# Sample states updated by VectorE beside the output and channel products, in a hybrid attention decoder layer

## Chip, cores and metric

The kernel runs on one NeuronCore of a Trainium2 chip. The metric is the device time of one execution in microseconds (us). TensorE is called PE below, its weight loads PEld, VectorE DVE, ScalarE ACT, GpSimd POOL, and SyncE, which issues nearly all DMAs, SP.

## What is computed

One decoder layer for 256 prompt tokens and 8 samples of 4 tokens each (288 tokens together), all in float32, model width 2048. After an RMSNorm, one input projection gives the operands of two branches and their gates. Branch A is sliding-window attention. Branch B is gated linear attention (GLA) with 4 heads, key width 256, value width 512 and a matrix state of 256 x 512 per head. For the samples, the states come in as an input and go out updated:

```
def step(S, xs):                      # one chunk; for a sample one chunk is its 4 tokens
    qc, kc, vc, dc = xs
    o = einsum('blhk,bhkv->blhv', qc, S)
    S = dc[..., None] * S + einsum('blhk,blhv->bhkv', kc, vc)
    return S, o
...
y = sigmoid(gs) * (o_swa @ p_swa) + sigmoid(gg) * (o_g @ p_gla)
x = x + y @ w_o
h2 = rms_norm(x, norm2)
x = x + square(relu(h2 @ w_up)) @ w_down
```

There are 8 samples x 4 heads = 32 sample states of 512 KB each. The state is used twice: `o` needs the product of the queries with the old state, and the new state is the decayed old one plus the sum over 4 tokens of key times value.

## The kernel before

All arrays are kept transposed, features on the 128 partitions and the 288 tokens along the free axis. All large products go through `gemm`. One `gemm` makes 512 output features; its weights come in chunks of 512 KB (`raw`, 128 x 1024, six buffers, loaded at L228 by SP), each chunk being two halves of 128 input rows. `wsplit` parts each half into a high part (`whi`, a rounding copy by ACT at L213) and a remainder (`wlo`, a subtraction by DVE at L155), five buffers of each. PE then does 24 matmuls for a chunk (L246): 2 halves x 4 output blocks x 3 products (high x high, high x low, low x high), all in the rounded float32 format. The four output banks (`mm`, four buffers) are read out by an `evac` function when the last chunk has been multiplied. The gemms follow each other in a fixed order: the input projections, `ps0..3` (attention's projection), more input projections (`gg`, `rg`: the gates), `pg0..3` (GLA's projection), `wo0..3` (output), and then four blocks of `up` and `dn` (the channel products), four gemms each.

All other work is put between chunks. `queues[0]` and `queues[1]` hold generators; after each chunk `pump(rate)` adds a rate to each queue's credit and runs one step (up to the next `yield`) of that queue for each whole credit. `gla(h)` is the prompt part of head h on queue 0; `gla_sample(h)` is its sample part on queue 1. The issue order on each engine is then set by the framework's scheduler, which takes what is ready by its own reckoning, the earliest traced first; `keep_in_program_order` pins an instruction behind the one traced before it on its engine.

`gla_sample(h)` does, before the change: the head's sample values in four copies are turned by PE (L787) and parted into `vs`; decays are made by ACT (`es`); the keys are weighted in four copies (`kdr`), turned by PE (L813) and parted into `kh`; then, two samples at a visit, two old states are loaded into `raw` buffers (L823), multiplied by the padded queries into the bank `pos` (L841), and for each of the two samples the keys of that sample are masked (`km`, L847, DVE), two matmuls make the new contribution (`pu`, L851) and DVE adds it to the decayed state in place (L852), which SP writes out (L853). After the four visits one matmul adds the part of the tokens within the sample (L855). Where the prompt part of the same head has its products ready (`tiled`), they are emitted beside a visit's matmuls. At the end the head's output is normalised by `rsqrt_mean` (L276 to L281), whose logarithm and exponential need another ACT function table than the sigmoids of `rg_evac` (L932); for head 3 `exp_table()` (L180) loads it, pinned.

The state writes and loads share SP's queue and the `raw` buffers with the weights.

Of the kernel before, what the change touches and what calls it, by code (L numbers as in the profile page):

```python
# [19 lines left out]
P = 128  # L20
D = 2048
KT = 16
TP = 256
# [5 lines left out]
GATE = 1.0 / 16.0  # L29
NEG = -1e30  # L30
# [100 lines left out]
def step_kernel(ctx: ExitStack, tc: tile.TileContext, a: dict):  # L131
# [36 lines left out]
    raw0 = main.tile([P, 1024], F32, name="raw", tag="raw", bufs=6)  # L168
# [48 lines left out]
    def gemm(name, xh, xl, evac, rate=(), first=None):  # L217
        nk = 2 * chunks_of(name)
        ps = [pmm.tile([P, 512], F32, name="mm", tag="mm") for _ in range(4)]
        for c in range(nk // 2):  # L220
            if FIRST[name] + c == 0:
                raw = raw0
            else:
                raw = main.tile([P, 1024], F32, name="raw", tag="raw", bufs=6)
# [12 lines left out]
            turns = c == nk // 2 - 1 or c == 0 and first is None  # L237
            order = [(i, m) for m in range(4) for i in range(2)] if turns else [(i, m) for i in range(2) for m in range(4)]
            order = [(i, m, j) for i, m in order for j in range(3)]
            if c == 0 and first is not None:  # L240

                order[:12] = [(0, m, j) for j in range(3) for m in range(4)]
            for i, m, j in order:
                k, hi, lo = parts[i]
                o, sl = ps[m][:, :NT], slice(m * P, m * P + P)
                T.matmul(o, lhsT=(lo if j == 2 else hi)[:, sl], rhs=xl(k) if j == 1 else xh(k),  # L246
                         start=k == 0 and j == 0, stop=k == nk - 1 and j == 2)
                if k == nk - 1 and j == 2:
                    evac(m, o)
            pump(rate)  # L250
# [14 lines left out]
    def rsqrt_mean(accs, n, out, ps=None):  # L265
# [10 lines left out]
        S.activation(t, ps[:, :NT], AF.Ln, scale=1.0 / n, bias=epst)  # L276
        V.tensor_scalar(m, ps[:, :NT], 1.0 / n, EPS, ALU.mult, ALU.add)
        S.activation(out, t, AF.Exp, scale=-0.5)
# [106 lines left out]
    def swa(pool):  # L385
        rope = pool.tile([P, 2, NT], F32, name="rope")
        vc1 = pool.tile([P, NB, P], F32, name="vc1")
# [119 lines left out]
        vc = [main.tile([P, NB, P], F32, name="vc0", tag="Zb3"), vc1]  # L507
# [73 lines left out]
    zqk, zv, og, ready, done, last_operands, tiled = {}, {}, {}, {}, set(), [], []  # L581
# [27 lines left out]
    ats = gpool.tile([P, 64], F32R, name="ats")  # L609
    V.memset(qm, 0.0)  # L610
    V.memset(f(ats), 0.0)
    bmask, amask, ii = bm[:, 32:32 + NB], bm[:, 0:32], bm[:, 32 + NB:64 + NB]
# [13 lines left out]
    def gla(h):  # L626
# [9 lines left out]
        vr = gpool.tile([P, 4, 4, TS], F32, name="vr")  # L636
        G.tensor_copy(vr, zv[h][:, :, TP:NT].unsqueeze(2).broadcast_to([P, 4, 4, TS]))
# [9 lines left out]
        ready[h] = (vr, pfx)  # L647
# [87 lines left out]
        tiled.append((products, lambda: cross(1)))  # L735
        for _ in range(8):
            if tiled:
                yield
# [40 lines left out]
    def gla_sample(h):  # L779
        zk = lambda t: zqk[h][:, 2 + t]  # L780
        while h not in ready:
            yield
        vr, pfx = ready[h]
        vs = gpool.tile([P, 512], F32R, name="vs")
# [3 lines left out]
        S.copy(vs, pv)  # L788
        sub(vs[32:64], pv[32:64], f(vs[32:64]))
        sub(vs[96:128], pv[96:128], f(vs[96:128]))  # L790
        yield
        ps = pfx[:, :, TP:NT]
# [9 lines left out]
        kdr = gpool.tile([P, 2, 4, TS], F32, name="kdr")  # L802
        mul(qi, zqk[h][:, 0:2, TP:NT], es[:, :, 0:TS])
        mul(kir, zqk[h][:, 2:4, TP:NT], ens)
        for t in range(2):
            kb = zk(t)[:, TP:NT].unsqueeze(1).broadcast_to([P, 4, TS])
            mul(kdr[:, t], kb, es[:, t, TS:64].unsqueeze(1).broadcast_to([P, 4, TS]))
        qd = qm.rearrange("p a (b c) -> p a b c", c=36)
        S.copy(qd[:, :, :, 0:NS], qi.rearrange("p a (b c) -> p a b c", c=NS))
        yield  # L810
        pk = bank("pks")
        for t in range(2):
            T.transpose(pk[:, P * t:P * t + P], kdr[:, t].rearrange("p a b -> p (a b)"), ident)  # L813
        kh = gpool.tile([P, 256], F32R, name="kh", tag="kh")
        S.copy(kh, pk[:, :256])
        sub(kh[64:128], pk[64:128, :256], f(kh[64:128]))
        yield
        pos = pos_.tile([P, 512], F32, name="pos", tag="pos")
        for b0 in range(0, NB, 2):
            st = []  # L820
            for b in (b0, b0 + 1):
                raw = main.tile([P, 1024], F32, name="raw", tag="raw", bufs=6)
                SY.dma_start(raw, a["s0"][h, b])  # L823
                st.append(raw)
            if b0 == 0:

                pa2 = bank("pa2")
                for t in range(2):
                    for g in range(4):
                        T.matmul(pa2[32 * g:32 * g + 32, :TS], lhsT=kir[:, t], rhs=qi[:, t], start=t == 0, stop=t == 1)  # L830
                at2 = gpool.tile([P, TS], F32, name="at2")
                mul(at2, pa2[:, :TS], amask)
                S.copy(ats[:, 0:TS], at2)
                sub(ats[64:128, 0:TS], at2[64:128], f(ats[64:128, 0:TS]))
            beside = tiled.pop() if tiled else (lambda: None, lambda: None)
            beside[0]()

            for g in range(2):
                for t in range(2):
                    r = 32 * (2 * g + t)  # L840
                    T.matmul(pos[r:r + 32], lhsT=qm[:, t, 32 * (b0 + g):32 * (b0 + g) + 32],  # L841
                             rhs=st[g][:, 512 * t:512 * t + 512], start=b0 == 0, stop=b0 == NB - 2 and r >= 64)
            beside[1]()
            for g in range(2):
                b, raw = b0 + g, st[g]
                km = gpool.tile([P, 256], F32R, name="km", tag="km")
                V.tensor_scalar(km, f(kh), bmask[:, b:b + 1], None, ALU.mult)  # L847
                for t in range(2):
                    rt = raw[:, 512 * t:512 * t + 512]
                    pu = bank("pu")  # L850
                    T.matmul(pu, lhsT=km[:, P * t:P * t + P], rhs=vs, start=True, stop=True)  # L851
                    V.scalar_tensor_tensor(rt, rt, es[:, t, NS * b + NS - 1:NS * b + NS], pu, ALU.mult, ALU.add)  # L852
                SY.dma_start(a["ssn"][h, b], raw)  # L853
                yield
        T.matmul(pos[:64], lhsT=ats, rhs=vs, start=False, stop=True)  # L855
# [24 lines left out]
        if h == 3:  # L880
            exp_table()
        rsqrt_mean([acc], 512, rso)
# [8 lines left out]
    R = (1.0, 0.55)  # L891
# [23 lines left out]
    R3 = (0.9, 0.55)  # L915
# [8 lines left out]
    for h in range(4):  # L924
# [3 lines left out]
        def rg_evac(m, ps):  # L928
# [6 lines left out]
            S.copy(gh[h][:, m], tt[:, m])  # L935
        gemm(f"rg{h}", H, L, rg_evac, rate=R3)
# [38 lines left out]
    def wo_evac(j):  # L975
# [6 lines left out]
        return evac  # L982
    for j in range(4):
        gemm(f"wo{j}", lambda k: yh[:, k], lambda k: yl[:, k], wo_evac(j))

    def norm2():
# [11 lines left out]

    rest = flat(big("YA", "parts", F32R))
    vh, vl, kh3, kl3 = (rest[:, i:i + n].rearrange("p (a b) -> p a b", a=2)  # L1000
                        for i, n in ((0, 1024), (1024, 1024), (2048, 512), (2560, 512)))

    def last_parts():
        vt, kdt = last_operands
# [7 lines left out]
    for blk in range(4):  # L1012
# [12 lines left out]
        for j in range(4):  # L1025
            gemm(f"up{blk}_{j}", lambda k: h2h[k // 4][:, k % 4], lambda k: h2l[k // 4][:, k % 4], up_evac(j),
                 rate=(1,) if blk == 0 and j == 0 else ())

        def dn_evac(j):
            def evac(m, ps):  # L1030
                i = 4 * j + m
                add(x1[:, i], ps, x1[:, i])
                if blk == 3:
# [11 lines left out]
                    S.mul(x1[:, i], x1[:, i], fn[:, i:i + 1])  # L1045
# [6 lines left out]
    rsqrt_mean(last[2:], D, rstd3, ssq3)  # L1052
    for t in range(2):

        pst = pmm.tile([P, 512], F32, name="mm", tag="mm")
        for i, (blk, k, v) in enumerate((blk, k, v) for blk in range(2) for k, v in ((kh3, vh), (kh3, vl), (kl3, vh))):
            T.matmul(pst, lhsT=k[:, blk, P * t:P * t + P], rhs=v[:, blk], start=i == 0, stop=i == 5)
# [4 lines left out]
    for n in (1, 1, 2, 2, 2, 2, 2, 2, 1, 1):  # L1062
        sl = slice(i, i + n)
        mul(x1[:, sl], x1[:, sl], rstd3.unsqueeze(1).broadcast_to([P, n, NT]))
# [83 lines left out]
```

## Time and profile before

| | |
|---|---|
| median of 3 runs | 1790.3 us (1789.91 to 1790.46) |
| the profiled execution | 1790.24 us |
| its span, first to last instruction | 1788.5 us |
| mean granted PE clock | 0.997 |
| PE / PEld busy | 1773.5 us (99%) / 1736.7 us (97%) |
| DVE / ACT / POOL busy | 1098.0 us (61%) / 843.4 us (47%) / 68.2 us (4%) |
| moved by DMA | 324.13 MB, mean 181 GB/s |

Busy time of PE counts matmuls whose modelled ends overlap: a 128x288 matmul is listed with 295 ns, but they start some 133 ns apart, so that a chunk of 24 takes 3.18 us. "Idle before" in a row is the time in which the engine stood still ahead of those instructions, with what ended it. The stages: swa attention to about 217 us, the GLA heads and their samples from about 225 to 710 us, `pg` and `wo` to about 959 us, then up and dn to 1774 us.

### The profile page before, as it was taken

The page shows a single profiled execution, that of the slowest core. Times are in us where ns is not written, and L with a number is a line of the kernel's source. Part 1 is how long each engine was busy: PE and PEld are TensorE (multiplying, and loading weights), DVE is VectorE, ACT ScalarE, POOL GpSimd, SP SyncE. Part 2 cuts the span into 40 slices and gives each one's busy share as a digit, 9 for nine tenths or more (in the row PEclk, how much of TensorE's full clock was granted, in tenths as well). Part 3 has the DMA queues.
Part 4 walks back from the last instruction along what each step waited for, and adds up shares of the span by engine and source line. Part 5 has one row for each costly group of instructions (what it writes and reads, how often), then busy time and mean ns, then how long its engine had stood idle before and what let it go on. Part 6 is the DMA issues. An engine that isn't in the chain of part 4 may idle for free.

```text
span 1788.5 us, 34299 instructions
## 1 busy us (share of the span) xinstructions
PE 1773.5 (99%) x13531; PEld 1736.7 (97%) x13531; DVE 1098.0 (61%) x2108; ACT 843.4 (47%) x1595; POOL 68.2 (4%) x79
## 2 busy tenths in 40 slices
PE   9999999999999999999999999999999999999997
PEld 8999998999989999999999999999999999999997
DVE  8896585685765867656666555455544554455544
ACT  6555454443533546544444553345433553345443
POOL 0000000101001001000131000000000000000010
PEclk9999999999999999999999999999999999999999
DMA  8634357476476475555545444544444444444442
GB/s 290 241 130 161 137 187 271 153 249 220 163 272 205 163 264 167 173 174 167 214 160 177 166 166 158 173 165 166 162 169 165 165 165 165 165 166 166 164 167 99
DMA packets 93473, 324.13 MB, mean 181 GB/s; under 512 B 11392, under 2 KB 13952, under 8 KB 93312
## 3 DMA queue, kind: packets, MB, share of 16 engines
q1 hardware_dynamic: 92736, 320.90, 52.0%
q8 instruction: 106, 1.74, 0.4%
q10 hardware_dynamic: 576, 1.05, 0.2%
q14 instruction: 55, 0.45, 0.1%
HBM read 298.25 MB, written 23.66 MB: 180 GB/s over the span
## 4 chain that ended last, share of the span: by engine, by line
PE 96%; DVE 2%; ACT 1%; issue 0%; DVEq 0%; ACTq 0%
PE mm L246 91%; PE pu L851 1%; PE pos L841 1%; PE pst L773 1%; DVE wlo L155 0%; PE score L443 0%; PE po L761 0%; PE o L487 0%; PE pt L475 0%; DVE x L149 0%; PE warm L367 0%; PE os L563 0%; PE po L762 0%; DVE e L149 0%; PE ssq L255 0%
## 5 line engine op out<-in xcount | busy, mean ns | idle before, releaser
L155 DVE TENSOR_TENSOR wlo<-raw,whi 128x512 fp32r<-128x512 f32 x1040 | 714.1, 699 | 584.4 <-ACT whi L213 582.1
L213 ACT CAST whi<-raw 128x512 fp32r<-128x512 f32 x1040 | 630.4, 619 | 799.6 <-PE mm L246 752.2
L246 PE MATMUL mm<-hh,whi 128*128 128x288 f32 x1472 | 439.7, 299 | 2.5 <-ACT whi L213 2.5
L246 PE MATMUL mm<-hl,whi 128*128 128x288 f32 x1472 | 434.0, 295 | 0.0
L246 PE MATMUL mm<-hh,wlo 128*128 128x288 f32 x1472 | 433.1, 295 | 0.0
L246 PE MATMUL mm<-uh,wlo 128*128 128x288 f32 x1024 | 301.9, 295 | 0.0
L246 PE MATMUL mm<-h2h,wlo 128*128 128x288 f32 x1024 | 301.9, 295 | 0.0
L246 PE MATMUL mm<-h2l,whi 128*128 128x288 f32 x1024 | 301.7, 295 | 0.0
L246 PE MATMUL mm<-ul,whi 128*128 128x288 f32 x1024 | 301.6, 295 | 0.0
L246 PE MATMUL mm<-h2h,whi 128*128 128x288 f32 x1024 | 301.6, 295 | 0.0
L246 PE MATMUL mm<-uh,whi 128*128 128x288 f32 x1024 | 301.6, 295 | 0.0
L246 PEld LDWEIGHTS mm<-hh,whi 128*128 128x128 f32 x1472 | 277.2, 188 | 7.4 <-ACT whi L213 3.2
L246 PEld LDWEIGHTS mm<-hl,whi 128*128 128x128 f32 x1472 | 277.2, 188 | 2.3 <-issue 0.7
L246 PEld LDWEIGHTS mm<-hh,wlo 128*128 128x128 f32 x1472 | 276.5, 188 | 0.3 <-issue 0.3
L246 PEld LDWEIGHTS mm<-h2h,wlo 128*128 128x128 f32 x1024 | 192.3, 188 | 0.0
L246 PEld LDWEIGHTS mm<-uh,wlo 128*128 128x128 f32 x1024 | 192.3, 188 | 0.0
L246 PEld LDWEIGHTS mm<-ul,whi 128*128 128x128 f32 x1024 | 192.1, 188 | 0.0
L246 PEld LDWEIGHTS mm<-h2l,whi 128*128 128x128 f32 x1024 | 192.1, 188 | 0.0
L246 PEld LDWEIGHTS mm<-uh,whi 128*128 128x128 f32 x1024 | 192.0, 188 | 0.0
L246 PEld LDWEIGHTS mm<-h2h,whi 128*128 128x128 f32 x1024 | 192.0, 188 | 0.0
L246 PE MATMUL mm<-yh,wlo 128*128 128x288 f32 x256 | 75.5, 295 | 0.0
L246 PE MATMUL mm<-gh,wlo 128*128 128x288 f32 x256 | 75.4, 295 | 0.0
(280 smaller groups left out, 1738.4 us busy)
## 6 DMA issues: line engine op xcount, KB each, us to landing
raw<-in_w SPq DMA_DIRECT2D x518, 512.0 KB, 3.3
raw<-in_s SPq DMA_DIRECT2D x32, 512.0 KB, 3.9
out_ssn<-raw SPq DMA_DIRECT2D x32, 512.0 KB, 4.2
x<-in_x SPq DMA_DIRECT2D x4, 576.0 KB, 5.7
x<-in_x SPq DMA_DIRECT2D x6, 288.0 KB, 7.5
out_y<-x SPq DMA_DIRECT2D x6, 288.0 KB, 2.6
out_sp<-so SPq DMA_DIRECT2D x6, 256.0 KB, 3.2
kc<-in_kc SPq DMA_DIRECT2D x2, 512.0 KB, 5.6
```

What stands on the lines that cost most here:

```text
L155: eng.tensor_tensor(out, x, y, ALU.subtract)
L213: S.copy(hi, raw)
L246: T.matmul(o, lhsT=(lo if j == 2 else hi)[:, sl], rhs=xl(k) if j == 1 else xh(k), start=k == 0 and j == 0, stop=k == nk - 1 and j == 2)
L773: T.matmul(pst, lhsT=kdt[:, blk, P * t:P * t + P], rhs=vt[:, blk], start=blk == 0, stop=blk == 1)
L841: T.matmul(pos[r:r + 32], lhsT=qm[:, t, 32 * (b0 + g):32 * (b0 + g) + 32], rhs=st[g][:, 512 * t:512 * t + 512], start=b0 == 0, stop=b0 == ...
L851: T.matmul(pu, lhsT=km[:, P * t:P * t + P], rhs=vs, start=True, stop=True)
```

## The change

The new states are no longer made by PE in `gla_sample`. There, a head's sample values are turned once (four matmuls into 32 rows, `vf`) and written to a DRAM tile `vd`; the decayed keys (`kdk`) and the decays (`dec`) of all heads are kept in SBUF. A visit now takes four samples, the four old states are only read, and it waits until the prompt part of its head has its products ready (`shown`). The tokens' own part becomes four matmuls of 128 columns.

A new generator `state_updates` on queue 1 runs from `wo0` on. For each of the 32 states it loads that sample's 4 x 512 values from `vd`, broadcast to all 128 partitions (1 MB, two buffers, in the place of `ya`), and the old state for the second time. ACT multiplies the first token's values by its key column, DVE adds the other three tokens (for each of the two 128-row halves) and then adds the decayed state: 2 ACT and 8 DVE instructions of 128x512 for a state, in 8 steps, one DVE instruction a step. The rates are 0.6 steps a chunk in `wo`, 0.96 in `up`, 1.22 in `dn`; what is left is drained before `dn3_0`.

Besides: `raw` has seven buffers; `vc1` shares the buffer `tt`; queue 1 has rate 0.7 instead of 0.55 in the GLA stage; head 3's `rsqrt_mean` starts two steps into or after `rg2`'s gemm (`late`) with its table load, logarithm and exponential pinned in order; the parts of the last prompt state are allocated later; in the last gemm the factor `fn` is applied by DVE at the very end instead of by ACT; and the first matmul of the last prompt states (L1057) is pinned behind the last sums of squares.

```diff
+RAW = 7
...
-    raw0 = main.tile([P, 1024], F32, name="raw", tag="raw", bufs=6)
+    raw0 = main.tile([P, 1024], F32, name="raw", tag="raw", bufs=RAW)
...
+        ln = S.activation(t, ps[:, :NT], AF.Ln, scale=1.0 / n, bias=epst)
+        if pinned:
+            tc.keep_in_program_order(ln)
...
+        ex = S.activation(out, t, AF.Exp, scale=-0.5)
+        if pinned:
+            tc.keep_in_program_order(ex)
...
     def gla_sample(h):
...
-            T.transpose(pv[:, P * j:P * j + P], vr[:, j].rearrange("p a b -> p (a b)"), ident)
+            T.transpose(pv[:TS, P * j:P * j + P], zv[h][:, j, TP:NT], ident)
+        S.copy(vf, pv[:TS])
+        SY.dma_start(vd[h], vf)
...
+        mul(kdk[:, h], zqk[h][:, 2:4, TP:NT], es[:, :, TS:64])
+        V.tensor_copy(dec[:, h], es[:, :, NS - 1:TS:NS])
...
+        while h not in shown:
+            yield
...
-        for b0 in range(0, NB, 2):
+        for b0 in (0, 4):
+            st = load_states(b0)
...
+            if b0 == 4:
+                for j in range(4):
+                    T.matmul(pos[32 * j:32 * j + 32, P * j:P * j + P], lhsT=at2, rhs=vf[:, P * j:P * j + P],
+                             start=False, stop=False, skip_group_check=True)
+            for i in range(0, 4, 2):
+                for g in range(2):
+                    for t in range(2):
+                        r, b = 32 * (2 * g + t), b0 + i + g
+                        T.matmul(pos[r:r + 32], lhsT=qm[:, t, 32 * b:32 * b + 32], rhs=st[i + g][:, 512 * t:512 * t + 512],
+                                 start=b < 2, stop=b >= NB - 2)
...
-                V.tensor_scalar(km, f(kh), bmask[:, b:b + 1], None, ALU.mult)
-                for t in range(2):
-                    T.matmul(pu, lhsT=km[:, P * t:P * t + P], rhs=vs, start=True, stop=True)
-                    V.scalar_tensor_tensor(rt, rt, es[:, t, NS * b + NS - 1:NS * b + NS], pu, ALU.mult, ALU.add)
-                SY.dma_start(a["ssn"][h, b], raw)
-        T.matmul(pos[:64], lhsT=ats, rhs=vs, start=False, stop=True)
...
         if h == 3:
+            while not late:
+                yield
+            yield
             exp_table()
-        rsqrt_mean([acc], 512, rso)
+        rsqrt_mean([acc], 512, rso, pinned=h == 3)
...
+    def state_updates():
+        vb = flat(big("YA", "vb"))[:, 0:4096].rearrange("p (a b) -> p a b", a=2)
+        items = [(h, b) for h in range(4) for b in range(NB)]
+        def load_values(i):
+            h, b = items[i]
+            SY.dma_start(vb[:, i % 2], vd[h, 4 * b:4 * b + 4].rearrange("a b -> (a b)").unsqueeze(0).broadcast_to([P, 2048]))
+        load_values(0)
+        paced = tc.keep_in_program_order
+        for i, (h, b) in enumerate(items):
+            acc = []
+            for t in range(2):
+                k = lambda n: kdk[:, h, t, NS * b + n:NS * b + n + 1]
+                v = lambda n: vb[:, i % 2, 512 * n:512 * n + 512]
+                acc.append(gpool.tile([P, 512], F32, name="acc_s", tag="AF"[t]))
+                S.mul(acc[t], v(0), k(0))
+                for n in range(1, NS):
+                    paced(V.scalar_tensor_tensor(acc[t], v(n), k(n), acc[t], ALU.mult, ALU.add))
+                    yield
+                    if t == 0 and n == 2 and i + 1 < len(items):
+                        load_values(i + 1)
+                    if t == 0 and n == 3:
+                        raw = main.tile([P, 1024], F32, name="raw", tag="raw", bufs=RAW)
+                        SY.dma_start(raw, a["s0"][h, b])
+            for t in range(2):
+                rt = raw[:, 512 * t:512 * t + 512]
+                paced(V.scalar_tensor_tensor(rt, rt, dec[:, h, t, b:b + 1], acc[t], ALU.mult, ALU.add))
+                if t == 1:
+                    SY.dma_start(a["ssn"][h, b], raw)
+                yield
+    queues[1].append(state_updates())
-        gemm(f"wo{j}", lambda k: yh[:, k], lambda k: yl[:, k], wo_evac(j))
+        gemm(f"wo{j}", lambda k: yh[:, k], lambda k: yl[:, k], wo_evac(j), rate=(0, 0.6))
...
-                 rate=(1,) if blk == 0 and j == 0 else ())
+                 rate=(1 if blk == 0 and j == 0 else 0, 0.96))
...
+                drain(1)
-            gemm(f"dn{blk}_{j}", lambda k: uh[:, k], lambda k: ul[:, k], dn_evac(j), rate=(1,))
+            gemm(f"dn{blk}_{j}", lambda k: uh[:, k], lambda k: ul[:, k], dn_evac(j), rate=(1, 1.22))
```

More of the change, by code (lines that the diff above doesn't have):

```diff
@@ L263, in square_sums_in_parts, with rsqrt_mean @@
         T.matmul(ps[:, :NT], lhsT=onesr, rhs=lo, start=False, stop=stop)
-    def rsqrt_mean(accs, n, out, ps=None):
+    def rsqrt_mean(accs, n, out, ps=None, pinned=False):
         if ps is None:
@@ L506, in swa @@
             yield
-        vc = [main.tile([P, NB, P], F32, name="vc0", tag="Zb3"), vc1]
+        vc = [main.tile([P, NB, P], F32, name=f"vc{p}", tag=t) for p, t in ((0, "Zb3"), (1, "tt"))]
         for p in range(2):
@@ L579, in step_kernel @@
     gemm("q0", H, L, scaled(lambda m: qp[0][:, m]))
-    zqk, zv, og, ready, done, last_operands, tiled = {}, {}, {}, {}, set(), [], []
+    zqk, zv, og, ready, done, shown, last_operands, tiled, late = {}, {}, {}, {}, set(), set(), [], [], []
     def gla_gemms(h, rate):
@@ L828, in gla_sample @@
                 for t in range(2):
[L829 to L834, printed above, removed]
+                    T.matmul(pa2[:TS, :TS], lhsT=kir[:, t], rhs=qi[:, t], start=t == 0, stop=t == 1)
@@ L835, in gla_sample @@
+                mul(at2, pa2[:TS, :TS], bm[:TS, 0:32])
             beside = tiled.pop() if tiled else (lambda: None, lambda: None)
             beside[0]()
[L838 to L842, printed above, removed]
-            beside[1]()
@@ L935, in rg_evac @@
             S.copy(gh[h][:, m], tt[:, m])
+        if h == 2:
+            late.append(True)
         gemm(f"rg{h}", H, L, rg_evac, rate=R3)
@@ L997, in step_kernel @@
     last = []
-    rest = flat(big("YA", "parts", F32R))
-    vh, vl, kh3, kl3 = (rest[:, i:i + n].rearrange("p (a b) -> p a b", a=2)
-                        for i, n in ((0, 1024), (1024, 1024), (2048, 512), (2560, 512)))
+    parts3 = []
     def last_parts():
+        rest = flat(big("YA", "parts", F32R))
+        parts3.extend(rest[:, i:i + n].rearrange("p (a b) -> p a b", a=2)
+                      for i, n in ((0, 1024), (1024, 1024), (2048, 512), (2560, 512)))
+        vh, vl, kh3, kl3 = parts3
         vt, kdt = last_operands
@@ L1056, in step_kernel @@
         for i, (blk, k, v) in enumerate((blk, k, v) for blk in range(2) for k, v in ((kh3, vh), (kh3, vl), (kl3, vh))):
-            T.matmul(pst, lhsT=k[:, blk, P * t:P * t + P], rhs=v[:, blk], start=i == 0, stop=i == 5)
+            mm = T.matmul(pst, lhsT=k[:, blk, P * t:P * t + P], rhs=v[:, blk], start=i == 0, stop=i == 5)
+            if i == 0:
+                tc.keep_in_program_order(mm)
         so = gpool.tile([P, 512], F32, name="so", tag="AF"[t])
@@ L1063, in step_kernel @@
         sl = slice(i, i + n)
-        mul(x1[:, sl], x1[:, sl], rstd3.unsqueeze(1).broadcast_to([P, n, NT]))
+        if i < 12:
+            mul(x1[:, sl], x1[:, sl], rstd3.unsqueeze(1).broadcast_to([P, n, NT]))
+        else:
+            for k in range(i, i + n):
+                V.scalar_tensor_tensor(x1[:, k], x1[:, k], fn[:, k:k + 1], rstd3, ALU.mult, ALU.mult)
         SY.dma_start(a["y"][:, sl], x1[:, sl])
```

64 lines of the change are left out of this document (22 added, 42 removed).

## Prediction

> **What bounds the kernel now.** I read the engines' shares and the chain that ended last on the page first.
>
> ```profile
> PE 1773.5 (99%) x13531; PEld 1736.7 (97%) x13531; DVE 1098.0 (61%) x2108; ACT 843.4 (47%) x1595; POOL 68.2 (4%) x79
> ...
> PE 96%; DVE 2%; ACT 1%; issue 0%; DVEq 0%; ACTq 0%
> PE mm L246 91%; PE pu L851 1%; PE pos L841 1%; PE pst L773 1%; DVE wlo L155 0%; PE score L443 0%; PE po L761 0%; PE o L487 0%; PE pt L475 0%; DVE x L149 0%; PE warm L367 0%; PE os L563 0%; PE po L762 0%; DVE e L149 0%; PE ssq L255 0%
> ```
>
> PE is the bound nearly from end to end: the chain runs 96% on it, and a matmul taken out shortens the span as long as nothing else becomes late. Then I asked for the busy time of three stretches: the GLA stage with the sample visits, nine microseconds at its end, and a stretch of the channel products. The columns are stretch, length, busy time of PE, PEld, DVE, ACT and POOL with instruction counts, granted PE clock, DMA share, GB/s.
>
> ```profile
> core 0 of [0], span 1788.5 us
> ...
> 225.00:705.00 480.00, 478.59 (x3742) 451.93 (x3742) 327.39 (x705) 222.10 (x407) 29.33 (x31) 1.00 0.62 214
> 705.00:714.00 9.00, 6.50 (x37) 6.27 (x37) 8.44 (x16) 6.92 (x12) 0.00 (x0) 0.81 0.14 45
> 1264.00:1366.00 102.00, 102.00 (x771) 102.00 (x770) 51.73 (x84) 41.30 (x71) 0.00 (x0) 1.00 0.48 166
> ```
>
> PE is full in the visits' stage and in the channel products, and in the latter DVE, ACT and the DMA engines stand still half the time: that is where the change puts its new work. The middle row is the one place where PE was starved (6.50 of 9.00 us) and slow (clock 0.81).
>
> **What leaves PE.** The chain through one pair of samples (start, length, what):
>
> ```profile
> 262.70 1.00 PE pos L841 x8
> 263.70 0.67 PE pu L851 x2
> 264.37 6.37 PE mm L246 x48
> 270.74 0.47 PE pu L851 x2
> ```
>
> A sample's two `pu` matmuls take 0.47 us between products, and 0.67 right after `pos`, of which 0.20 is thus the tail of `pos`. All 32 samples: 32 x 0.47 = 15.0 us saved, and between that and 16 x (0.67 + 0.47) = 18.2 if the tails went too. The tails stay once a visit. `pos` itself stays: 16 visits x (1.00 + 0.20) = 19.2 us become 8 visits of two sets, 8 x (2.00 + 0.20) = 17.6; I take 1.6 us saved, with ends of 0 (each set keeps its tail) and 3.2 (none is left).
>
> Two smaller pieces, as PE's order of time shows them (start, duration):
>
> ```profile
> 243.51 0.38 PE L813 MATMUL pks<-ident,kdr 128*128 128x128 f32 x2
> ```
>
> ```profile
> 311.45 0.79 PE L855 MATMUL pos<-vs,ats 128*64 128x512 f32 x1
> 312.09 0.29 PE L246 MATMUL mm<-hh,whi 128*128 128x288 f32 x1
> ```
>
> The key transposes go: 4 heads x 0.38 = 1.5 us at most, since the 0.38 holds the last one's pipeline end; I take 0.6 (ends 0 and 1.5). The tokens' own part held PE 0.64 us a head, 2.6 in all; in its place come four matmuls of 128 columns, between nothing and the same 0.64; I take half, 1.3 us saved (ends 0 and 2.6). The value transposes stay sixteen in number, narrower, and I cost them at no change; so the token products (a quarter of them left, but the four groups ran side by side).
>
> **The starved place.** The chain from 690 to 720 us, by line, and PE behind the gap:
>
> ```profile
> by line: PE mm L246 68.3%; ACT gh L935 5.0%; ACT L276 4.3%; ACT L932 4.3%; ACT L278 4.3%; ACT L180 4.3%; ACT whi L213 4.2%; ACT sr L932 2.6%; issue 2.5%; ACT rs_t L276 0.6%; ACT rso L278 0.1%; ACTq L213 0.1%
> ```
>
> ```profile
> 708.70 0.40 PE L246 MATMUL mm<-hh,whi 128*128 128x288 f32 x1 [2.50 <-ACT whi L213]
> ...
> 710.26 0.44 PE L246 MATMUL mm<-hl,whi 128*128 128x288 f32 x1
> 710.50 0.44 PE L246 MATMUL mm<-hh,wlo 128*128 128x288 f32 x1
> ```
>
> Four pieces of 4.3% of 30 us, 1.29 us each, carry ACT with no operand: function tables loaded in turn, since head 3's logarithm and exponential (L276, L278) fell among the four sigmoids that read out `rg1` (L932). For over 5 us ACT rounded no weights, PE ran out of them for 2.50 us, and then its matmuls started 0.24 us apart instead of 0.13 until the clock came back. Cost: 2.50 + 9.00 x (1 - 0.81) = 4.2 us. After the change I count the steps: at 0.7 a chunk head 3's last step comes two to three chunks into `rg2`, 16 us ahead of its sigmoids, pinned as one group: one load there, one at `rg2`'s sigmoids. I take 4.2 us saved; ends 0 (the stall moves to `rg2`) and 4.2. The Trainium skill, TensorE: Matmul & The Clock Gate, "What's actually happening", lets the clock drop after an idle window of about 3.4 us; by that alone a gap of 2.5 us need not slow PE, the piece would be 2.5 and the total 1.7 us smaller, but here the 0.81 row decides.
>
> Sum on PE: 15.0 + 1.6 + 0.6 + 1.3 + 4.2 = 22.7 us; ends 15.0 (the `pu` matmuls alone) and 15.0 + 3.2 + 1.5 + 2.6 + 4.2 = 26.5 (the tails behind `pos` stand in the 3.2).
>
> **What is added, and what covers it.** Durations of the nearest kinds (busy, mean ns | idle before):
>
> ```profile
> L155 DVE TENSOR_TENSOR wlo<-raw,whi 128x512 fp32r<-128x512 f32 x1040 | 714.1, 699 | 584.4 <-ACT whi L213 582.1
> L213 ACT CAST whi<-raw 128x512 fp32r<-128x512 f32 x1040 | 630.4, 619 | 799.6 <-PE mm L246 752.2 <-DMA raw<-in_w 28.3 <-DVE wlo L155 5.4
> ...
> L852 DVE SCALAR_TENSOR_TENSOR raw<-raw,es,pu 128x512 f32<-128x512 f32 x64 | 44.8, 742 | 15.5 <-PE pu L851 15.2
> ...
> L1020 DVE SCALAR_TENSOR_TENSOR ur<-mm,rstd 128x288 f32<-128x288 f32 x64 | 29.2, 456 | 6.9 <-PE mm L246 6.6
> ```
>
> DVE: 32 x 8 operations of the L852 kind, 256 x 0.742 = 190 us, against 64 of them and the masks taken out. In an `up` gemm (8 chunks x 3.18 = 25.4 us) DVE has 16 x 0.699 = 11.2, some 8 x 0.456 = 3.6 of read-out and new 7.7 x 0.742 = 5.7: 20.5 us, 81%. In `dn`: 11.2 + 1.8 + 9.8 x 0.742 = 20.3, 80%. It fits. ACT: 64 more of about 0.62 us, 40 us over 800; from 41.30/102 to some 45%. Cover: ACT waited 752.2 us for PE to give back a `whi` buffer, so the split runs its five halves, 8 us, ahead; one 0.74 us operation between two subtractions is hidden. Without that lead each would cost up to 0.74 us, 190 us in all.
>
> New waits on DVE: a state's first sum waits for ACT's product and that for the 1 MB broadcast, its last two for the second load of the state; behind a late one queue the `wlo` of the next chunks, and PE waits for those 8 us later. The broadcast is issued six steps ahead, 6 x 3.18 / 0.96 = 20 us in `up` and 16 in `dn`; the state three steps, 10 and 8 us. How long do loads take?
>
> ```profile
> q1 hardware_dynamic: 92736, 320.90, 52.0%
> ...
> raw<-in_w SPq DMA_DIRECT2D x518, 512.0 KB, 3.3
> raw<-in_s SPq DMA_DIRECT2D x32, 512.0 KB, 3.9
> out_ssn<-raw SPq DMA_DIRECT2D x32, 512.0 KB, 4.2
> x<-in_x SPq DMA_DIRECT2D x4, 576.0 KB, 5.7
> ```
>
> A state lands in 3.9 us, within 8. The 1 MB broadcast does not occur before; from below, all traffic ran at 52.0% x 1788.5 / 320.9 = 2.9 us a MB, 3.0 us of the engines; from above, x's 576 KB took 5.7 us, 10.1 us for 1 MB. I take 3.0, the row with contiguous runs of some KB like these. Then an `up` period (one state, 8.3 chunks, 26.5 us) has 12.7 us of weights (0.48), 1.5 + 1.5 of state in and out, 3.0 of broadcast: 18.7, 71%; `dn` (6.6 chunks, 20.9 us) 16.0, 77%. The visits' stage, which ran at 0.62 with both directions, loses the writes.
>
> Moved DMAs, all on SP: 32 state writes out of the GLA stage, 32 second loads, 32 broadcasts and 4 small value writes. A state's write waits in SP's queue for DVE's last sum (one 0.742 us operation) and its buffer is held until that write has landed (4.2 us more); the seventh buffer makes up for it, and SP is six chunks or so ahead. In a visit SP spends four free buffers on states, each freed about once a chunk, and falls back to two or three chunks of lead, 6 to 10 us against 3.3 us of landing: cost 0, with an end of 3.9 us x 8 visits = 31 (rival 3). POOL loses four copies. `vc1`'s load now waits for the rounded keys to be read, as `vc0`'s does already: nothing.
>
> The tail, from PE's order of time and the groups:
>
> ```profile
> 1775.65 0.60 PE L1057 MATMUL mm<-parts 128*128 128x512 f32 x1
> 1776.10 0.42 PE L255 MATMUL ssq<-sqf,ones 128*128 128x288 f32 x1
> ```
>
> ```profile
> L884 DVE SCALAR_TENSOR_TENSOR og<-og,norms,rso 128x288 f32<-128x288 f32 x16 | 7.2, 515 | 0.0
> ...
> L149 DVE TENSOR_TENSOR x<-x,rstd 128x576 f32<-128x576 f32 (+1 forms) x10 | 5.6, 634 | 0.0
> ```
>
> A matmul of the last states no longer stands ahead of the last sum of squares (0.45 us saved at most); the last four rows, a quarter of 5.6 us, become 4 x 0.515 = 2.1 (0.7 lost at most). I take 0.2 lost.
>
> Forecast: the profiled execution's 1790.24 us, 0.06 under the median of 1790.3, less 22.7 and plus 0.2 = 1767.7 us. With the ends of the PE sum alone it would be 1775.4 and 1763.9.
>
> **The rivals.**
> 1. *The broadcast is slow, and DMA becomes the bound (slower).* All 128 rows read the same 8 KB, which no row of the trace does. In `dn` a period leaves 20.9 - 10.0 - 3.0 = 7.9 us for it, in `up` 10.8. At the upper end of 10.1 us the 14.6 states updated in `dn` lose 2.2 us each, 32 us: 1767.7 + 32 = 1799.7. It eats the whole gain from 7.9 + 22.5 / 14.6 = 9.4 us on. Against it: the 2.9 us a MB. The Trainium skill, DMA: Bandwidth & Descriptors, "Latency and other measured facts", reports 103 GB/s where all partitions' streams stand on rows a large power of two apart and infers that they meet on the same memory channels; a pitch of zero could be such a case, and 1 MB would then take an estimated 10.2 us. No row here shows it.
> 2. *DVE is late at the gemms' ends (no change).* The four `mm` banks must be read out before the next gemm's products; an update ahead of the first read-out in each of the 32 gemms with updates costs 0.742: 23.7 us, 1791.4. Against: 80% load, and a read-out that is traced earlier than the update behind it. Half of it, or as much of scattered small waits, gives 1771 to 1779.
> 3. *Four loads at once starve a visit.* Half the landing time of the last one, 2 us x 8 visits: 1783.7. For it: 0.62 share in that stage; against: the 28.3 us that ACT waited for weights there reached PE nowhere.
> 4. *The visits' pace was not PE's.* Then only the 4.2 us of the tables come: 1786. Against: PE busy 478.59 of 480.
>
> **Chances and numbers.** Forecast (1763 to 1771) 0.68; small waits (1771 to 1779) 0.13; rival 3 0.05; rival 4 0.02; rival 2 in full 0.04; rival 1 0.08. The range 1763 to 1779 holds 0.81. A measurement of this kernel tells 0.2%, 3.6 us, from no change: faster 0.68 + 0.13 + 0.05 + 0.01 = 0.87, same 0.05, slower 0.08.
>
> **What would show it.** `pu`, `km` and the key transposes gone, `pos` as eight groups of some 2.2 us; one table load in `rg2` and no PE gap near 690 us; DVE near 77% and DMA near 0.7 in the channel products with PE at 102.00 of 102.00; broadcast landing under 8 us. Wrong: a broadcast over 9 us, ACT waiting for weights in `dn`, PE rows with "<-DVE wlo" or "<-DVE x" ahead of products, or gaps ahead of `pos`.

## The result, and the profile after

| | before | after |
|---|---|---|
| median, beside each other on one chip | 1790.11 us (1789.36 to 1790.46) | 1773.88 us (1773.43 to 1774.47) |
| span of the profiled execution | 1788.5 us | 1771.9 us |
| DVE / ACT / POOL busy | 61% / 47% / 4% | 68% / 49% / 4% |

The change saves 16.2 us: ratio 0.9911, 95% interval [0.9897, 0.9925]. The forecast was 1767.7, with a gain of 22.4; 1773.9 lies in its range, in the bracket of "small waits", which had a chance of 0.13. The question of the experiments is thus where 6 us went.

The engines' shares, the DMA queue and the chain that ended last, on the page of after:

```profile
PE 1755.6 (99%) x13439; PEld 1722.8 (97%) x13439; DVE 1206.2 (68%) x2252; ACT 876.1 (49%) x1644; POOL 62.5 (4%) x75
...
q1 hardware_dynamic: 102144, 371.49, 59.3%
...
PE 97%; DVE 1%; POOL 1%; DMA 1%; ACT 0%; issue 0%; DVEq 0%; SPq 0%
```

PE still carries the chain. New in it are DMA with 1%, which lies in the first 11 us, and POOL with 1%, at three places between 303 and 545 us; the chain of before named neither. The same stretches as in the prediction, and the output products in between (stretch, length, busy time of PE, PEld, DVE, ACT, POOL, clock, DMA share, GB/s):

```profile
225.00:705.00 480.00, 475.73 (x3750) 453.44 (x3750) 287.48 (x614) 226.62 (x411) 23.57 (x28) 1.00 0.53 185
857.00:943.00 86.00, 85.65 (x645) 85.42 (x644) 66.05 (x100) 42.92 (x75) 24.48 (x27) 1.00 0.65 230
...
1264.00:1366.00 102.00, 102.00 (x771) 102.00 (x770) 74.39 (x119) 45.18 (x74) 0.00 (x0) 1.00 0.74 267
```

In the channel products all went as forecast: PE is full at 102.00 of 102.00, DVE went from 51.73 to 74.39 us (73%), the DMA engines from 0.48 to 0.74. What was lost, was lost earlier: PE stands still for 4.3 of 480 us in the GLA stage (1.4 before), and for 0.35 of 86 in the output products.

The starved place, ACT's table loads in order of time and the stretch around them:

```profile
689.58 1.28 ACT L181 ACT_TABLE_LOAD   x1
...
709.05 1.28 ACT L928 ACT_TABLE_LOAD   x1
```

```profile
690.00:714.00 24.00, 24.00 (x183) 24.00 (x182) 17.84 (x34) 14.50 (x26) 0.00 (x0) 1.00 0.46 155
```

One load in `rg2` and one at its sigmoids, no gap and full clock. The loads and stores of the states (KB each, median us from issue to landing):

```profile
raw<-in_w SPq DMA_DIRECT2D x518, 512.0 KB, 3.9
raw<-in_s SPq DMA_DIRECT2D x64, 512.0 KB, 3.5
vb<-vd SPq DMA_DIRECT2D x32, 1024.0 KB, 6.3
```

The broadcast lands in 6.3 us, under the 8 named. Now the waits of PE (who waited for what, us, times, longest):

```profile
PE mm L247 <- DVE zqk L593: 4.3, 3, 1.4
...
PE mm L247 <- DVE wlo L156: 0.9, 3, 0.3
```

Neither stood in the profile of before. The first is a read-out: the first product of `v1`, `v2` and `v3` needs a bank that DVE has not yet read out from `qk1`, `qk2` and `qk3` (`zqk`, L593). The chain through the first of these three places (start, length, what):

```profile
303.27 0.82 POOL acc_o L153
...
304.16 1.49 POOL sqo L150
...
306.67 0.81 POOL acc_o L153
...
307.50 0.44 ACT ss_h L261
...
307.97 0.04 DVE ss_l L156
308.00 0.34 issue
308.34 0.46 DVE zqk L593
```

POOL adds up the squares of the previous head's output (`sqo`, `acc_o`); ACT rounds the sum (`ss_h`), DVE takes the remainder (`ss_l`); and the read-out that PE needs stands behind `ss_l` in DVE's queue. PE's last product before was issued at 307.24, the next at 308.94. DVE's own order of time there:

```profile
303.30 1.34 DVE L156 TENSOR_TENSOR wlo<-raw,whi 128x512 fp32r<-128x512 f32 x1 [1.40 <-ACT whi L214]
304.67 1.25 DVE L156 TENSOR_TENSOR w<-w2r,w 32x256 fp32r<-32x256 f32 x1
305.93 0.81 DVE L639 TENSOR_SCALAR w<-w,bm 32x256 fp32r<-32x256 f32 x1
306.78 0.98 DVE L640 SCALAR_TENSOR_TENSOR w<-w2r,bm,w 32x256 fp32r<-32x256 f32 x1
307.97 0.46 DVE L156 TENSOR_TENSOR ss_l<-acc_o,ss_h 128x288 fp32r<-128x288 f32 x1 [0.21 <-ACT ss_h L261]
```

Two things lie on top of each other: DVE's queue waits for POOL's sums, and DVE's operations beside POOL's are two to three times as long (`w` 1.25 us, and 0.42 in the kernel before). The chain goes by the sums: DVE was through with its own work 0.21 us before `ss_l` could begin. The kernel before had the same sums and the same wait at another place:

```profile
320.01 1.45 POOL L149 TENSOR_TENSOR sqo<-og 128x576 f32<-128x576 f32 x1 [38.60 <-DVE og L863]
...
326.17 0.46 DVE L155 TENSOR_TENSOR ss_l<-acc_o,ss_h 128x288 fp32r<-128x288 f32 x1 [4.16 <-ACT ss_h L260]
```

There DVE stood still for 4.16 us, but in the middle of a gemm, after `qk1` had been read out (from 307.94 on): only weight remainders were behind it in the queue, and the split's lead covered them.

### The profile page after: what moved, and what is told of

Same layout as the page of the kernel before. It is cut to its first block, busy times and chain, and to the rows that moved or that the text cites. A ratio compares the mean times of both kernels' runs of the same rounds, so it can differ in the third digit from the quotient of the medians.

```text
span 1771.9 us, 34406 instructions
## 1 busy us (share of the span) xinstructions
PE 1755.6 (99%) x13439; PEld 1722.8 (97%) x13439; DVE 1206.2 (68%) x2252; ACT 876.1 (49%) x1644; POOL 62.5 (4%) x75
## 4 chain that ended last, share of the span: by engine, by line
PE 97%; DVE 1%; POOL 1%; DMA 1%; ACT 0%; issue 0%; DVEq 0%; SPq 0%
PE mm L247 92%; PE pos L843 1%; PE pst L777 1%; DMA raw<-in_w 1%; POOL acc_o L153 0%; PE score L447 0%; PE po L765 0%; PE o L491 0%; PE pt L479 0%; DVE wlo L156 0%; POOL sqo L150 0%; DVE x L150 0%; PE os L567 0%; PE po L766 0%; PE pv L660 0%
## 5 line engine op out<-in xcount | busy, mean ns | idle before, releaser
L247 PE MATMUL mm<-h2h,wlo 128*128 128x288 f32 x1024 | 302.0, 295 | 0.3 <-DVE wlo L156 0.3
L1001 DVE SCALAR_TENSOR_TENSOR acc_s<-vb,kdk,acc_s 128x512 f32<-128x512 f32 x192 | 144.5, 759 | 0.1
```

The costliest lines, as they stand in the source:

```text
L1001: paced(V.scalar_tensor_tensor(acc[t], v(n), k(n), acc[t], ALU.mult, ALU.add))
```

## The experiments

Theory A: the loss is the place of POOL's sums. The visits have other steps than before, and the head's normalisation now meets the end of the next `qk` gemm. Rival B: it is the order of DVE's own work there, the gate operand `w` (four instructions, of which three are DVE's) having come ahead of the read-out.

The first 77 us, which no edit touches, differ by up to 1.2 us between the traced executions of the changed kernels. Differences of a microsecond or less are therefore read from the starts of the same PE matmuls in two traces.

**The sums on VectorE** (squares_by_dve): POOL has no part in it, the order on PE stays.

```
-            mul(sq, o_g[:, 2 * i:2 * i + 2], o_g[:, 2 * i:2 * i + 2], G)
+            mul(sq, o_g[:, 2 * i:2 * i + 2], o_g[:, 2 * i:2 * i + 2], V)
...
-                add(acc, sq[:, 0], sq[:, 1], G)
+                add(acc, sq[:, 0], sq[:, 1], V)
...
-                add(acc, acc, sq[:, 0], G)
-                add(acc, acc, sq[:, 1], G)
+                add(acc, acc, sq[:, 0], V)
+                add(acc, acc, sq[:, 1], V)
```

> The changed kernel with the squares and sums of a head's output (sqo, acc_o) made by VectorE instead of GpSimd; PE's order is the same. Theory A: no operation of VectorE is slowed (the parting of w 1.25 us instead of 3.0) and ss_h comes some 2 us earlier; VectorE has 2.9 us more of its own, some of it in the 1.4 us in which it waited: the stalls shrink from 1.6 to under 0.6 us each, 3 to 5 us less than the changed kernel, 1769 to 1771. Theory B (order alone): with 2.9 us more ahead of the read-out the stalls grow, 1774 to 1778.

Measured: 1768.13 us (1767.91 to 1768.28), ratio to before 0.9879 [0.9866, 0.9893]; span 1766.3. This is 5.7 us less than after, somewhat more than the 3 to 5 of theory A. By the starts of PE's matmuls 5.3 us come back at the three places, and 0.3 lie in the first 77 us. PE's waits for `zqk` are gone, and `w` has its old lengths (min/median/max ns over the four heads; in after the medians are 1253, 808 and 974):

```profile
L156 DVE TENSOR_TENSOR w<-w2r,w x4: 407/417/417, 220.4 to 538.8; 32x256 fp32r<-32x256 f32 x4
L639 DVE TENSOR_SCALAR w<-w,bm x4: 352/352/354, 220.8 to 543.4; 32x256 fp32r<-32x256 f32 x4
L640 DVE SCALAR_TENSOR_TENSOR w<-w2r,bm,w x4: 484/484/485, 221.9 to 543.8; 32x256 fp32r<-32x256 f32 x4
```

**The sums later** (late_turn): three more steps ahead of the head's turning back, so that POOL's sums fall into the next gemm again, on POOL.

```
+        for _ in range(3 if h < 3 else 0):
+            yield
         pt = bank("pt2")
```

> The changed kernel with three more yields ahead of the turning of a head's sample output (pt2) for heads 0 to 2. In the changed kernel's trace PE stands still three times for 1.6 us (at 307, 426 and 545 us), each time at the first matmul of a v gemm. Theory A: GpSimd's sums of squares (sqo, acc_o) for the head's normalisation now fall on the end of the qk gemm; they slow VectorE and make ss_h and ss_l wait, and these stand ahead of the read-out of the output banks (zqk). Moved some four chunks later, into the middle of the v gemm, they should cost nothing: 5.0 us less than the changed kernel, about 1769. Theory B: it is the parting of the next head's gate weights (w), brought forward by the scheduler, that is ahead of the read-out whatever GpSimd does: the stalls stay, about 1773 to 1774.

Measured: 1768.49 us (1768.07 to 1768.64), ratio 0.9881 [0.9866, 0.9896]; span 1766.9. Place alone suffices. POOL's first sum of squares moved from 302.0 to 315.1 us, and the stretch in which PE had stood still is full:

```profile
300.00:310.00 10.00, 10.00 (x72) 9.52 (x71) 5.99 (x12) 3.38 (x6) 0.00 (x0) 1.00 0.46 154
310.00:325.00 15.00, 15.00 (x116) 15.00 (x115) 7.66 (x12) 6.14 (x11) 5.35 (x5) 1.00 0.44 149
```

**The gate operand pinned** (pinned_gate): its four instructions keep the order of the program.

```
-        S.copy(w2, w2r)
-        sub(w2[64:96], w2r[64:96], f(w2[64:96]))
+        pin = tc.keep_in_program_order
+        pin(S.copy(w2, w2r))
+        pin(V.tensor_tensor(w2[64:96], w2r[64:96], f(w2[64:96]), ALU.subtract))
...
```

> The changed kernel with the four instructions that part the gate weights (w) pinned in program order, so that they no longer run at the end of the qk gemm. Theory A: ss_l still waits for GpSimd's sums through ss_h (which ended at 307.94 us, with the read-out at 308.34), so the stalls stay: within 1.5 us of the changed kernel's 1773.9. Theory B: the three stalls go, about 1769.

Measured: 1775.45 us (1775.24 to 1777.78), ratio 0.9925 [0.9912, 0.9937]; no gain, so B falls; it is 1.6 us more than after, where theory A had allowed 1.5. In its trace `w` no longer stands there and has its short lengths, yet the waits of PE grew:

```profile
PE mm L247 <- DVE zqk L593: 6.3, 3, 2.1
```

```profile
307.68 0.46 DVE L156 TENSOR_TENSOR ss_l<-acc_o,ss_h 128x288 fp32r<-128x288 f32 x1 [3.26 <-ACT ss_h L261]
308.20 0.69 DVE L156 TENSOR_TENSOR wlo<-raw,whi 128x512 fp32r<-128x512 f32 x1
308.81 0.82 DVE L593 SCALAR_TENSOR_TENSOR zqk<-mm,rstd 128x288 f32<-128x288 f32 x2
```

DVE stood idle for 3.26 us ahead of `ss_l`, with a weight remainder and then the read-out queued behind it. So the longer `w` is not needed for the stall. That the wait for `ss_l` is enough by itself is not shown here: the chain that ended last goes through that remainder and its weights.

```profile
304.45 3.13 DMA raw<-in_w
307.57 0.60 ACT whi L214
```

ACT began to round these weights at 307.56, as soon as it had taken up `ss_h` (307.22), and they landed at that same time: two waits ended together. The remainder kept DVE 0.6 us ahead of the read-out, about as much as PE waited longer than in after, where the read-out came first (308.34, the remainder 308.71).

**The sums on VectorE in the kernel before** (before_squares): the control. The edit is that of squares_by_dve.

> The kernel before with the sums of squares of the heads' outputs on VectorE instead of GpSimd, nothing else. If these sums cost PE something only where they meet a gemm's end, as the theory has it, they cost nothing here, where they stand in the middle of the next gemm: 1789 to 1791 us, while the same edit in the changed kernel took 5.7 us off. If VectorE's operations beside GpSimd's cost PE time wherever they stand, the edit brings part of that here too: 1785 to 1787.

Measured: 1790.09 us (1789.36 to 1790.39), ratio 1.0000 [0.9991, 1.0009]. What is worth 5.7 us after the change is worth nothing before it.

**No updates in the output products** (no_updates_in_wo):

```
-        gemm(f"wo{j}", lambda k: yh[:, k], lambda k: yl[:, k], wo_evac(j), rate=(0, 0.6))
+        gemm(f"wo{j}", lambda k: yh[:, k], lambda k: yl[:, k], wo_evac(j))
...
-                 rate=(1 if blk == 0 and j == 0 else 0, 0.96))
+                 rate=(1 if blk == 0 and j == 0 else 0, 1.11))
```

> The changed kernel with no state updates beside the output products (wo); the up products take them at 1.11 steps a chunk instead of 0.96. If the two PE gaps of 0.51 us in wo come from update sums ahead of wlo on VectorE, they go: 1.0 us less, about 1772.9, with VectorE's busy share in up higher by a seventh of the updates' part (from 20.5 to 21.4 us of 25.4) and still no gap there. If VectorE's margin is smaller than its busy share says, new gaps in up eat the 1.0 us or more: 1774 to 1778.

Measured: 1772.52 us (1772.38 to 1773.06), ratio 0.9904 [0.9889, 0.9919]; span 1770.8, 1.1 us less than after. Both gaps are gone, and the stretch behind them holds none (85.65 and 626.65 us of PE in after):

```profile
857.00:943.00 86.00, 86.00 (x650) 86.00 (x650) 57.31 (x85) 41.03 (x72) 24.89 (x28) 1.00 0.55 186
943.00:1570.00 627.00, 627.00 (x4725) 626.86 (x4725) 474.41 (x776) 311.50 (x550) 4.22 (x5) 1.00 0.74 261
```

In after, the second gap's neighbourhood on DVE and on POOL shows that POOL is in it again, here with the squares of the new activations:

```profile
945.08 2.37 DVE L1001 SCALAR_TENSOR_TENSOR acc_s<-vb,kdk,acc_s 128x512 f32<-128x512 f32 x2
947.37 1.29 DVE L156 TENSOR_TENSOR wlo<-raw,whi 128x512 fp32r<-128x512 f32 x1
```

```profile
944.92 0.91 POOL L153 TENSOR_TENSOR acc<-acc,sq 128x288 f32<-128x288 f32 x1
945.78 1.12 POOL L150 TENSOR_TENSOR sq<-x 128x288 f32<-128x288 f32 x1
```

Two updates of the usual 0.745 us took 2.37 together and the next remainder 1.29 instead of 0.69. That the gaps need POOL as well was not tried by itself; that they need the updates is shown.

**No multiply-adds** (no_sums): the 192 multiply-adds are left out (three of four products of each new state).

```
-                    paced(V.scalar_tensor_tensor(acc[t], v(n), k(n), acc[t], ALU.mult, ALU.add))
```

> The changed kernel without the six multiply-adds of each state's update (192 on VectorE in all; left out: three of the four products in each new state); product, decay, loads, broadcasts and writes stay. If VectorE's 145 us of sums are covered but for the two gaps in wo, as the forecast costed them but for those gaps, 1.0 us goes at most: 1772.5 to 1774. If they cost scattered small waits in up and dn, or hold back the weight split, more goes: 1771 or less.

Measured: 1772.75 us (1772.46 to 1773.92), ratio 0.9905 [0.9890, 0.9921]; DVE falls to 55.77 of 102.00 us in the channel products, and nothing is won beyond the two gaps. The 145 us of multiply-adds are covered but for about 1 us.

**More multiply-adds** (more_sums): each multiply-add of a state's first half twice (those three products are added twice).

```
+                    for _ in range(2 - t):
                         paced(V.scalar_tensor_tensor(acc[t], v(n), k(n), acc[t], ALU.mult, ALU.add))
```

> The changed kernel with each of the three multiply-adds of a state's first half issued twice (96 more operations of 0.76 us on VectorE, 73 us; it adds those three products twice). In a dn gemm VectorE goes from 20.3 to some 23.0 us of 25.4, in wo beyond what it has room for at the chunks where a state starts. If cover is a matter of the share, up and dn stay full and only the gaps in wo grow: 1774 to 1777. If VectorE has no margin left at 77%, PE waits for wlo in dn: 1780 or more, up to 1773.9 + 73.

Measured: 1774.41 us (1774.15 to 1774.98), ratio 0.9914 [0.9900, 0.9927]: 0.5 us more than after. With DVE at 82% PE is still full, and only the second gap in the output products grew (0.5 to 1.1 us, by the starts of PE's matmuls):

```profile
1264.00:1366.00 102.00, 102.00 (x771) 102.00 (x770) 83.47 (x134) 45.12 (x75) 0.00 (x0) 1.00 0.75 270
```

**Two broadcasts** (two_broadcasts): the second load writes the same values to the same place.

```
-            SY.dma_start(vb[:, i % 2], vd[h, 4 * b:4 * b + 4].rearrange("a b -> (a b)").unsqueeze(0).broadcast_to([P, 2048]))
+            for _ in range(2):
+                SY.dma_start(vb[:, i % 2], vd[h, 4 * b:4 * b + 4].rearrange("a b -> (a b)").unsqueeze(0).broadcast_to([P, 2048]))
```

> The changed kernel with each of the 32 broadcasts of 1 MB loaded twice into the same buffer. If a broadcast costs the DMA engines 3.0 us, as the forecast took it, a dn period goes from 16.0 to 19.0 of 20.9 us and an up period from 18.7 to 21.7 of 26.5: still covered, 1773.9 to 1776. If it costs them the 6.3 us that it takes to land, a dn period holds 10.0 + 3.0 + 12.6 = 25.6 us of work in 20.9, and the 14.6 states of dn lose up to 4.7 us each: up to 1842.

Measured: 1778.14 us (1776.63 to 1779.33), ratio 0.9935 [0.9922, 0.9947]: 4.3 us more than after, outside both expectations, though near the first. The queue's row and SP's order of time:

```profile
q1 hardware_dynamic: 106752, 405.05, 64.3%
```

```profile
844.32 12.52 SPq L990 DMA_DIRECT2D vb<-vd  x4
856.89 9.75 SPq L229 DMA_DIRECT2D raw<-in_w  x8
```

The engines' time rose from 0.593 x 1771.9 to 0.643 x 1776.3 us, by 91.4, or 2.86 us a broadcast: the 3.0 of the forecast, not the 6.3 of the landing. In the channel products PE stayed full, at a DMA share of 0.83. By the starts of PE's matmuls 3.6 of the 4.4 us between the spans were lost at one place: the first four broadcasts held SP's queue for 12.52 us, weights behind them came late, and PE stood still 2.9 us in three gaps from 862 to 872. The other 0.8 lie in the first 77 us. Since the doubled load must wait for the first one to the same buffer, this wait is partly the experiment's own.

**Two `pu` matmuls for one, in the kernel before** (two_pu):

```
-                    T.matmul(pu, lhsT=km[:, P * t:P * t + P], rhs=vs, start=True, stop=True)
+                    for _ in range(2):
+                        T.matmul(pu, lhsT=km[:, P * t:P * t + P], rhs=vs, start=True, stop=True)
```

> The kernel before with each of the 64 pu matmuls issued twice into the same bank. If PE sets the pace of the visits, as the forecast has it, 64 more pu matmuls cost 64 x 0.235 = 15.0 us by the chain's 0.47 us a pair, and up to 17.1 by the start-to-start time that pu took in the kernel before: 1804.6 to 1806.7 us. If DVE or the state loads set the pace (rival 4), the second matmul stands in a gap and the time stays near 1790.

Measured: 1803.68 us (1803.08 to 1804.22), ratio 1.0077 [1.0063, 1.0091]. The visits' pace is PE's: 13.6 us more, 0.9 under the range that was expected and a little under the 14.8 by which the `pu` matmuls themselves grew (from start to start 31.9 instead of 17.1). 14.8 / 64 = 0.23 us is the price of one that the forecast used. Two short waits of PE for `km`, 0.7 us in before, are gone; the rest of the difference is not followed up.

**Only the tables' part, in the kernel before** (before_tables): head 3's step waits for `rg2` and its two functions are pinned, as in the change; all else is the kernel before.

```
+            while not late:
+                yield
+            yield
...
-        rsqrt_mean([acc], 512, rso)
+        rsqrt_mean([acc], 512, rso, pinned=h == 3)
```

> The kernel before with only one part of the change: head 3's normalisation begins in rg2's gemm, its table load, logarithm and exponential pinned in order. Theory: the 2.5 us gap at 706 us and the slow matmuls behind it go, 4.2 us less than before, about 1786, two table loads less. Rival: the gap moves to rg2's or rg3's read-out and the time stays within 1 us of 1790.

Measured: 1786.17 us (1785.39 to 1786.71), ratio 0.9979 [0.9971, 0.9988], 3.5 us less than before at the medians; the span is 4.8 shorter, of which 0.6 lie in the first 77 us. The stretch from 690 us, of before and then of this kernel:

```profile
690.00:714.00 24.00, 21.50 (x151) 21.27 (x150) 18.71 (x36) 18.00 (x30) 0.26 (x1) 0.93 0.34 105
```

```profile
690.00:714.00 24.00, 24.00 (x183) 23.92 (x182) 18.57 (x34) 15.54 (x30) 0.00 (x0) 1.00 0.53 173
```

2.50 us of idle PE and 24 x 0.07 = 1.7 us of clock are back: 4.2. From start to start, too, PE's matmuls gain 4.2 us at this place.

**Both repairs** (both_mended): squares_by_dve and no_updates_in_wo together in the changed kernel.

> The changed kernel with both repairs: the sums of squares of the heads' outputs on VectorE instead of GpSimd, and no state updates beside wo (1.11 steps a chunk in up). If the three stalls of 1.6 us at the qk products' ends and the two of 0.5 us in wo are all that the additions cost, the time is 1768.1 - 1.0 = 1767.1 us, and PE shows no gap over 0.45 us behind the first 225 us but the last sum of squares. If the updates still cost something in up, it stays at 1768 or more.

Measured: 1767.40 us (1766.85 to 1767.49), ratio 0.9874 [0.9860, 0.9887]; span 1765.7. It is 6.5 us under after and the fastest of all. PE is full in the three stretches where it was not (475.73, 85.65 and 626.65 us in after):

```profile
225.00:705.00 480.00, 479.99 (x3790) 458.56 (x3789) 291.61 (x639) 230.54 (x415) 2.62 (x8) 1.00 0.56 187
857.00:943.00 86.00, 86.00 (x650) 86.00 (x649) 58.77 (x85) 39.74 (x70) 29.10 (x31) 1.00 0.52 176
943.00:1570.00 627.00, 627.00 (x4726) 626.86 (x4725) 473.07 (x776) 312.74 (x552) 0.00 (x0) 1.00 0.74 262
```

## Why the prediction was right, and where it was short

The terms, forecast against the trace (us saved; PE's matmuls from start to start, before against after, and where a kernel settles it, that kernel):

| step of the forecast | forecast | measured |
|---|---|---|
| `pu` gone 15.0, visits merged 1.6 | 16.6 | 17.1 + 1.0 = 18.1 |
| key transposes | 0.6 | 0.55 |
| the tokens' own part | 1.3 | 0.7 |
| the starved place | 4.2 | 4.2 (before_tables) |
| the tail, from the last product of `dn3_3` to the end | -0.2 | 0.0 (14.21 before, 14.25 after) |
| token products of the samples, and the prompt's matmuls beside them | 0 | -0.7 |
| new waits at the ends of `qk1` to `qk3` | 0 | -5.3 (squares_by_dve) |
| updates in the output products | 0 | -1.1 (no_updates_in_wo, spans) |
| sum | 22.5 | 16.5, against 16.6 of the spans |

- *What leaves PE* was right. The merging of the visits and `pu` can't be kept apart as neatly as it was done: the tails of `pos` stood partly in the `pu` rows. The tokens' own part was taken at half the span between its ends, and came nearer to the lower one. The token products, costed at no change, cost 0.4 more, and the `pa` matmuls beside them another 0.4, with 0.15 back at the prompt's `pv` and `pst`.
- *The starved place* was right in its cause and size; before_tables gives it by itself. The place where the clock fell to 0.81 is gone.
- *What covers the additions* was right for the channel products: DVE at 73% where 77% was named (the sums had given 80% and 81%), DMA at 0.74, broadcast 6.3 us, PE full. no_sums and more_sums show the cover from both sides: 145 us of multiply-adds less save about 1, 73 more cost 0.5. Rival 1 is out (2.86 us of the engines for a broadcast), and so is a bound by DMA. The Trainium skill's rule of a large power-of-two row pitch (DMA: Bandwidth & Descriptors, "Latency and other measured facts"), by which 1 MB would have taken an estimated 10.2 us, does not extend to a pitch of zero here: 6.3 us.
- Rival 4 is out by two_pu. Rival 3 is not seen: in both_mended, whose visits also take four loads, PE is busy 479.99 of 480 us.
- *The step that failed* is the count of steps. The prediction counted at 0.7 a chunk where head 3's logarithm and exponential would come, but not where the other three heads' normalisations would. In the kernel before, the sums of heads 0 to 2 began 12.1, 7.2 and 12.1 us behind the first read-out of the next `qk` gemm (320.01 behind 307.94 with the first); in after they began 6.3 us ahead of it each time (302.04 ahead of 308.34), and 5.3 us went there. Rival 2 had the right object, a read-out that is late on DVE, but the wrong cause and place: it put it to the updates, in gemms that have them; the stalls are in gemms without a single update, behind a wait for POOL. Its bracket of "small waits" held the time, for a reason that the text did not name: to that extent it was luck.
- *Updates hidden in the output products* was the second zero that failed, by 1.1 us. Their cost was worked out for `up` and `dn` only. In `wo` DVE has two operations of its own for each read-out (L153 and L978), and POOL's squares run beside them.

## What to carry to other kernels

A change in the number of steps moves all work that is queued behind these steps, not only the work that the change is about: for each piece that moves, look at which gemm's end it meets, and what stands behind its waits in an in-order queue. A wait of 4 us in DVE's queue cost nothing while only weight remainders with a lead were behind it, and 1.6 us of PE each time a bank's read-out was. An engine's free share in a stage of full cover can be given away nearly to the end (82% with PE still full); but where a gap opens, read the few microseconds ahead of it, not the share.

## What the runs showed of the hardware

VectorE slows beside GpSimd. With POOL's tensor operations running, `w` took 1253 ns instead of 417, `wlo` 1.3 us instead of 0.69. The Trainium skill, SBUF — State Buffer, "Who interferes with whom", says that a VectorE instruction with two SBUF inputs and a GpSimd instruction that reads SBUF exclude each other for a whole instruction. The trace agrees: `w` began at 304.67, while POOL's `sqo` ran from 304.16 to 305.65, and ended at 305.92, 0.27 us after it. Alone `w` takes 0.42 us, so the agreement is rough. The control before_squares shows that in the kernel before, where DVE had time to spare, POOL's sums cost nothing.

The clock survived shorter gaps than the one before the change. Behind 2.13 us of waiting in pinned_gate the granted clock stayed at 1.00:

```profile
548.28 0.37 PE L247 MATMUL mm<-hh,whi 128*128 128x288 f32 x1 [2.13 <-DVE zqk L593]
```

Behind the 2.50 us of before it fell, to 0.81 over nine microseconds: to 0.50 from 709.93 to 713.34, while the matmuls had begun again at 708.70. Both lie under the idle window of about 3.4 us that the Trainium skill gives (TensorE: Matmul & The Clock Gate, "What's actually happening"); where the limit lies between, and whether it lies at the same place each time, no run here shows.
